# Attention values product: native fp32 for three key tiles, three products of rounded halves for the other three

## The chip, the cores and the metric

The kernel runs on 1 core of one Trainium2 chip. The metric is device time in microseconds (us), and the time before is the median of three runs. A profile is one execution that the hardware profiler recorded; its own time and its span are given beside the median, because durations are read from it.

Five engines run side by side, each through its own instructions in order: TensorE multiplies matrices (PE in the profile, with its weight loads on a row of their own, PEld), VectorE (DVE) and ScalarE (ACT) work on rows of 128 partitions, GpSimd (POOL) does small things, and SyncE (SP) issues the loads. They wait for each other by semaphores.

## The reference, cut to what matters

Two layers over 512 latent tokens and 256 context tokens of width 1024: first a pooling mixer, then attention, each followed by a squared-ReLU MLP. The change lies in the attention of the second layer. Eight query heads of width 128 share two key/value heads, and each latent query sees all 768 tokens:

```python
def attend(q, k, v):
    s = jnp.einsum('bqhgd,bkhd->bhgqk', q, k).astype(jnp.float32) * (HEAD_DIM ** -0.5)
    p = jax.nn.softmax(s, axis=-1).astype(v.dtype)
    return jnp.einsum('bhgqk,bkhd->bqhgd', p, v)
```

The last line is the one that the change touches: probabilities times values, summed over the 768 keys, in six key tiles of 128. All of it is fp32.

## The kernel before, in words

**Two ways to multiply in fp32.** TensorE takes fp32 operands natively (tiles of type F32), or in a rounded form (F32R). With rounded operands one product loses low bits, so the kernel splits an operand x into hi, x rounded by a copy on ScalarE, and lo = x - hi by a subtraction on VectorE, and adds three products, hi*hi + hi*lo + lo*hi. Almost every product of this kernel is made of three such products. The attention values product was not: it was native.

**The attention.** A step is one head h and one block t of 128 queries; there are 32 steps, head by head, four blocks to a head (`steps`, line 1189). A step goes through four functions:

- `s_scores` (line 1200): six rounded matmuls of 384 columns into the PSUM tile `pss` (two 512-column banks, from a pool of two, `psA`); VectorE takes the maximum of each row (line 1212), ScalarE the exponential with its sum (line 1213), into one of four row buffers. In the trace these four are called `gate`, `p`, `p` and `acc`, in the order t = 0, 1, 2, 3.
- `s_norm` (line 1217): VectorE's reciprocal (1219) and the scaling of the 128x768 row (1220).
- `s_turn` (line 1222): TensorE transposes the six 128x128 key tiles of the row, three at a time, into a PSUM tile `pspt` (line 1230), and ScalarE copies each three to `soft["t"]`, called `pT` in the trace (line 1231).
- `s_values` (line 1233), once for two steps, so 16 times: for 256 queries, six native matmuls (line 1241), one for each key tile kt, add values times probabilities into a PSUM tile `po`. The stationary operand is a 128x128 tile of the values, kept in rows 4 and 5 of `xr`; the moving one is 128x256 of `pT`. ScalarE and VectorE then store hi and lo of the result (lines 1242 and 1243).

`pspt`, `po` and `pq` (below) come from one pool, `psB`, of four 512-column PSUM tiles. A tile is given to its next user when the last reader has finished.

Beside the steps, `q_head` (line 1192) transposes the queries of a head through `pq` and splits them (1197, 1198), and the output weights are loaded and split in quarters of 512 columns (lines 126 and 129).

**What sets the order.** Each function is put at a due time written out by hand (`attention`, line 1281): step i has its scores at i + 0.2, its scaling at i + 1.3, its transposes at i + 3.1, and the values of a pair at i + 5.2 of its second step, in units of 2.7. So the values of a pair are due after the transposes of the step two later. From the program in this order a planner then fixes, by its own estimates, each engine's final order of instructions; it may put a transpose between two matmuls of the scores. In the run itself each engine follows that order strictly.

**Where the values come from.** Ahead of the attention, `kv_a` projects 128 tokens to keys and values in a `psq` tile, `kv_e` (line 1079) copies the value half with ScalarE into `xr` (line 1081) and starts the norm of the keys; `head_norm` (from line 1033) finishes the keys on VectorE. The token tiles come in the order 4, 5, 0, 1, 2, 3.

**The ramp.** The last query projections (`project`, line 1021, and `head_norm`, lines 1037 to 1051) overlap the first steps of the attention, between 678 and 697 us of the span. VectorE has both kinds of work there.

Of the kernel before, what the change touches and what calls it, by code (L numbers as in the profile page):

```python
# [9 lines left out]
F32 = mybir.dt.float32  # L10
F32R = mybir.dt.float32r
BF16 = mybir.dt.bfloat16
AF = mybir.ActivationFunctionType
ALU = mybir.AluOpType
# [3 lines left out]
P = 128  # L18
D = 1024
KT = D // P  # L20
LAT = 512
# [3 lines left out]
NT = TOK // P  # L25
# [30 lines left out]
def backbone(ctx: ExitStack, tc, x, c, ctx_in, c_ctx, w_ada, b_ada, g_mix_pre, g_mix_post,  # L56
# [3 lines left out]
    sy, ve, sc, gp, te = nc.sync, nc.vector, nc.scalar, nc.gpsimd, nc.tensor  # L60
# [9 lines left out]
    def residents(stack):  # L70
        pool = stack.enter_context(tc.tile_pool(name="residents", bufs=1, side="right"))
        return (pool.tile([P, NT, D], F32, name="xr"), pool.tile([P, 2, D], F32, name="gate"),
                pool.tile([P, D], BF16, name="junk"))

    xr, gate, junk = residents(held[0])
# [15 lines left out]
    rb = const.tile([P, 10240], F32R, name="rb")  # L91
# [642 lines left out]
    for n, t in enumerate(order):  # L734
        b = 55 + 3 * n
# [289 lines left out]
    def head_rstd(ps, nh):  # L1025
        ss, ms, r = sm_tile("ss"), sm_tile("ms"), sm_tile("rs")
        for h in range(nh):
            sc.activation(junk[:, 0:HD], ps[:, h * HD:(h + 1) * HD], AF.Square, accum_out=ss[:, h:h + 1])
        gp.tensor_scalar(out=ms[:, 0:nh], in0=ss[:, 0:nh], scalar1=1.0 / HD, scalar2=EPS, op0=ALU.mult, op1=ALU.add)
        gp.tensor_tensor(out=r[:, 0:nh], in0=ms[:, 0:nh], in1=nhalf[:, 0:nh], op=ALU.pow)  # L1030
        return r
# [39 lines left out]
            if cols == THIRDS:  # L1071
                tc.keep_in_program_order(z)

    values = lambda: xr[:, 4:6].rearrange("p t n -> p (t n)")[:, 0:1536].rearrange("p (t n) -> p t n", n=256)

    def kv_a(t):
        pj[t] = project(t, chunks[2])

    def kv_e(t):
        ps = pj[t]  # L1080
        sc.copy(values()[:, t, :], ps[:, 256:512])
        pj[t] = ps, head_rstd(ps, NKV)

    def kv_b(t):
# [26 lines left out]
    def last0(st, n, t):  # L1111
# [5 lines left out]
        if n % 2:  # L1117
            st.at([18.2, 28.6, 39][n // 2], norm_pair, t - 1, 1, 0, hH, hL, True, (True, True, False)[n // 2],
                  ((True, False, False, False, False, False, False, True), (True, True, True, False, False, False, True, True), (True, False, True, False, True, False, True, False))[n // 2])
        st.at([31.4, 36.6, 41.8, 47, 55, 60.2][n], kv_a, t)  # L1120
        st.at([36.874, 40.793, 45.993, 51.193, 59.193, 65.4][n], kv_e, t)
        st.at([36.9, 42.1, 47.3, 52.5, 60.5, 65.7][n], kv_b, t)
        st.at([44.9, 50.1, 57.151, 62.351, 70.351, 75.551][n], kv_c, t)
# [44 lines left out]
    soft = {}  # L1168

    def open_soft():  # L1170
        uheld[0].close()
        pool = uheld[0].enter_context(tc.tile_pool(name="soft", bufs=1))
        qs = pool.tile([P, 2 * 1024], F32R, name="qs")
        qTs.extend((qs[:, 1024 * i:1024 * i + 512], qs[:, 1024 * i + 512:1024 * i + 1024]) for i in range(2))
        soft["t"] = pool.tile([P, NT, LAT], F32, name="pT")
        ps = [pool.tile([P, TOK], F32, name=f"p{i}") for i in range(2)]
        soft["p"] = ps

# [43 lines left out]
    def s_turn(i):  # L1222
        _, t = steps[i]
        sl = slice(t * P, (t + 1) * P)
        p = pbuf(i % 4)
        for b in range(2):
            ps = psB.tile([P, 3, P], F32, tag="b", name="pspt")
            for j in range(3):
                k = 3 * b + j
                te.transpose(ps[:, j, :], p[:, k * P:(k + 1) * P], ident)  # L1230
            sc.copy(soft["t"][:, 3 * b:3 * b + 3, sl], ps)

    def s_values(i):
        h, t = steps[i]
        half = t // 2
        kv = h // 4
        hs = slice(kv * HD, (kv + 1) * HD)
        qs = slice(256 * half, 256 * half + 256)
        po = psB.tile([P, 512], F32, tag="b", name="po")
        for kt in range(NT):  # L1240
            te.matmul(po[:, 0:256], values()[:, kt, hs], soft["t"][:, kt, qs], start=(kt == 0), stop=(kt == NT - 1))
        sc.copy(oH[:, h, qs], po[:, 0:256])
        ve.tensor_tensor(out=oL[:, h, qs], in0=po[:, 0:256], in1=oH[:, h, qs], op=ALU.subtract)

# [36 lines left out]
    def attention(st, base, unit_t):  # L1281
        at = lambda i, fn, *args: st.at(base + unit_t * i, fn, *args)
        for i, (h, t) in enumerate(steps):
            if t == 0:
                at([-2, 3, 4.542, 7.928, 13.236, 15.602, 19.752, 23.755][h], q_head, h)
            at(i + 0.2, s_scores, i)
            at(i + 1.3, s_norm, i)
            at(i + 3.1, s_turn, i)
            if t % 2:
                at(i + 5.2, s_values, i)  # L1290
        raws, late = [], []
        at(1.1, open_soft)
        at(37.5, close_soft)
        at(7, lambda: wo[0].append(wo_unit(0, 0, raws)))
        at(11.386, lambda: wo[0].append(wo_unit(0, 1, raws)))
        for n in range(8):
            at(9.05 + 2 * n, lambda n: split(*raws[n // 4], True, n % 4), n)
        for kk in range(2):
            at((23.386, 25.741)[kk], lambda kk: late.append(raw_load(w_o[1, kk], rawp)), kk)
            at(37.6, lambda kk: wo[1].append(aring.place(late[kk], 512, raws)), kk)  # L1300
        at(37.812, lambda: split(*raws[2], q=0))
        at(38.427, lambda: split(*raws[2], q=1))
        at(37.814, lambda: split(*raws[2], q=2))
        at(37.815, lambda: split(*raws[2], q=3))
        at(39.191, lambda: split(*raws[3], q=0))
        at(39.192, lambda: split(*raws[3], q=1))
        at(39.193, lambda: split(*raws[3], q=2))
        at(45.691, lambda: split(*raws[3], q=3))
        at(39.281, gate_diag if False else gate_rows, 1, GT1, 0)
# [118 lines left out]
```

## Time and profile before

| | |
|---|---|
| median of 3 runs | 1182.24 us (1181.07 to 1183.31) |
| the profiled execution, its own time | 1180.16 us |
| its span | 1178.3 us |
| the attention's values products, first start to last end | 697.7 to 786.9 us |
| native matmuls in them | 96, in the trace as 192 records |

In the page of the profile, part 1 gives the busy time of each engine. In a row of a group stand the line, the engine, the operation, the output and inputs, the shapes and the count, then the total busy time in us and the mean of one in ns, then the idle time of the engine just before, and what ended it. In a timeline, a row holds the start in us, the duration in us and the same names; instructions of one kind that follow each other are merged (x12), and durations of TensorE's rows reach beyond the start of the next, as matmuls are pipelined: the pace is read from starts. A native matmul of 256 columns leaves two records, a rounded one leaves one.

### The profile page before, as it was taken

What the parts mean: (1) busy time and instruction counts of PE and PEld (TensorE: products, weight loads), DVE (VectorE), ACT (ScalarE), POOL (GpSimd) and SP (SyncE); (2) the same over time, 40 slices, a digit from 0 to 9 for tenths busy, and PEclk for the clock granted to TensorE, in tenths of its full rate; (3) what the DMA queues carried; (4) which work ended last, traced back from release to release, by engine and by line L of the source; (5) the groups of instructions that cost most, each with busy time, mean ns of one, the idle gap of its engine ahead of it and who ended that gap; (6) DMA issues with size and microseconds to landing.
All of it is one profiled execution on the core that took longest, in us unless ns stands there. A gap on an engine that the chain in (4) does not pass through costs nothing.

```text
span 1178.3 us, 15759 instructions
## 1 busy us (share of the span) xinstructions
PE 1145.3 (97%) x6074; PEld 990.0 (84%) x6074; DVE 922.6 (78%) x1491; ACT 627.6 (53%) x1072; POOL 68.8 (6%) x120
## 2 busy tenths in 40 slices
PE   5799999999999999999999999999899999999997
PEld 4579888998889988998888889988888888888886
DVE  3787778998988998896777587657687779778876
ACT  3776654555354445555585367752676346435522
POOL 2030000000000000000242200001100000000001
PEclk9999999999999999999999999999999999999999
DMA  8984213334433334343423101115234124214312
GB/s 340 378 290 172 72 72 117 135 142 144 143 143 143 132 120 145 110 147 135 179 72 108 37 1 36 37 50 203 101 120 170 47 97 143 108 36 143 107 38 106
DMA packets 25643, 147.84 MB, mean 125 GB/s; under 512 B 2736, under 2 KB 5216, under 8 KB 9824
## 3 DMA queue, kind: packets, MB, share of 16 engines
q1 hardware_dynamic: 25568, 146.84, 34.2%
q8 instruction: 48, 0.79, 0.3%
q14 instruction: 27, 0.22, 0.1%
HBM read 139.49 MB, written 7.34 MB: 125 GB/s over the span
## 4 chain that ended last, share of the span: by engine, by line
PE 48%; issue 43%; DVE 4%; POOL 2%; ACT 2%; DMA 1%; SPq 0%; POOLq 0%; DVEq 0%; ACTq 0%
PE pso L776 22%; PE psin L677 18%; PE psq L1021 3%; PE psin L553 3%; POOL rs L171 1%; PE psada L226 1%; POOL rs L1030 1%; ACT junk L156 1%; PE psm L420 1%; PE pspool L480 1%; DVE xr L328 1%; POOL ms L169 0%; DMA xr<-in_ctx 0%; DMA xr<-in_x 0%; DVE rows L268 0%
## 5 line engine op out<-in xcount | busy, mean ns | idle before, releaser
L776 PE MATMUL pso<-units,rb 128*128 128x512 f32 x1152 | 278.8, 392 | 0.0
L776 PEld LDWEIGHTS pso<-units,rb 128*128 128x128 f32 x1152 | 214.7, 188 | 41.1
L268 DVE SCALAR_TENSOR_TENSOR rows<-raw,cond,rows 128x256 f32<-128x256 f32 x280 | 126.8, 476 | 2.0
L788 DVE TENSOR_TENSOR acc<-acc,pso 128x512 f32<-128x512 f32 x129 | 85.2, 675 | 41.9 <-PE pso L776 41.7
L553 PE MATMUL psin<-ra,rb 128*128 128x512 f32 (+1 forms) x432 | 104.7, 342 | 2.4 <-ACT ra L363 1.6
L880 PE MATMUL pso<-units,pairs 128*128 128x512 f32 x336 | 82.3, 389 | 0.0
L553 PEld LDWEIGHTS psin<-ra,rb 128*128 128x128 f32 x432 | 70.2, 189 | 13.6 <-ACT ra L363 1.9
L553 PE MATMUL psin<-ra 128*128 128x512 f32 x256 | 80.6, 390 | 0.0
L880 PEld LDWEIGHTS pso<-units,pairs 128*128 128x128 f32 x336 | 63.1, 188 | 13.1
L884 DVE TENSOR_TENSOR acc<-acc,pso 128x512 f32<-128x512 f32 x72 | 48.7, 682 | 28.8 <-PE pso L880 28.8
L169 POOL TENSOR_SCALAR ms<-ss 128x1 f32<-128x1 f32 x20 | 10.0, 502 | 1001.3 <-ACT junk L156 989.2
L677 PE MATMUL psin<-ra,units 128*128 128x384 f32 x336 | 65.6, 337 | 0.4 <-ACT psin L689 0.4
L677 PE MATMUL psin<-sums,units 128*128 128x384 f32 x336 | 64.0, 336 | 0.0
L677 PEld LDWEIGHTS psin<-ra,units 128*128 128x128 f32 x336 | 59.9, 188 | 3.9 <-ACT psin L689 0.5
L677 PEld LDWEIGHTS psin<-sums,units 128*128 128x128 f32 x336 | 58.9, 188 | 1.6
L129 DVE TENSOR_TENSOR units<-raw,units 128x1024 fp32r<-128x1024 f32 (+2 forms) x49 | 55.0, 1150 | 5.9 <-ACT units L126 5.6
L126 ACT CAST units<-raw 128x1024 fp32r<-128x1024 f32 (+2 forms) x49 | 47.0, 995 | 17.9 <-PE pso L776 13.7
L553 PEld LDWEIGHTS psin<-ra 128*128 128x128 f32 x256 | 48.0, 188 | 10.0
L553 PE MATMUL psin<-rb 128*128 128x512 f32 (+1 forms) x144 | 52.6, 367 | 0.2 <-DVE rb L364 0.2
L786 ACT COPY acc<-pso 128x512 f32<-128x512 f32 x48 | 27.1, 586 | 48.3 <-PE pso L776 47.8
L1021 PE MATMUL psq<-units,ra 128*128 128x512 f32 x216 | 51.6, 392 | 0.0
L553 PE MATMUL psin<-rb,ra 128*128 128x512 f32 x128 | 49.8, 389 | 0.0
(250 smaller groups left out, 2318.3 us busy)
## 6 DMA issues: line engine op xcount, KB each, us to landing
raw<-in_w_ada SPq DMA_DIRECT2D x48, 1024.0 KB, 4.9
raw<-in_w_mlp_in SPq DMA_DIRECT2D x32, 1024.0 KB, 4.9
raw<-in_w_mlp_out SPq DMA_DIRECT2D x32, 1024.0 KB, 5.2
raw<-in_w_qkv SPq DMA_DIRECT2D x6, 1024.0 KB, 4.8
spill<-xr SPq DMA_DIRECT2D x10, 512.0 KB, 9.0
xr<-spill SPq DMA_DIRECT2D x10, 512.0 KB, 6.7
raw<-in_w_o SPq DMA_DIRECT2D x4, 1024.0 KB, 4.8
xr<-in_x SPq DMA_DIRECT2D x4, 512.0 KB, 4.2
```

Source lines behind the costliest of these rows:

```text
L126: a = sc.copy(hi, raw)
L129: b = ve.tensor_tensor(out=lo, in0=raw, in1=hi, op=ALU.subtract)
L156: z = sc.activation(junk[:, 0:src.shape[-1]], src, AF.Square, scale=float(D) ** -0.5, accum_out=ss)
L268: ve.scalar_tensor_tensor(out=r, in0=raw[:, k, :], scalar=cond[:, k, c:c + 1], in1=r, op0=ALU.mult, op1=ALU.add)
L553: te.matmul(ps[:, bank, o:o + ln], w[:, k, fs], rhs, start=start, stop=(k == KT - 1 and n == 2), skip_group_check=len(ks) < KT)
L677: te.matmul(bank, w[k], a[k], start=start and k == 0 and m == 0, stop=stop and k == 3 and m == 2, skip_group_check=True)
L776: te.matmul(pss[h][:, 0:cols[h][1]], a[:, f, ts_], w[:, f, cols[h][0]:sum(cols[h])], start=(n == 0 and not seeded[t]), stop=(n == len(seq) ...
L786: sc.copy(d, ps)
L788: ve.tensor_tensor(out=d, in0=d, in1=ps[:, 0:w], op=ALU.add)
L880: te.matmul(ps, a, w, start=(m == 0), stop=(m == len(seq) - 1))
L884: ve.tensor_tensor(out=M[n][:, t], in0=M[n][:, t], in1=ps, op=ALU.add)
L1021: te.matmul(ps, a[:, k, sl], w[:, k % 4, :], start=(k == 0 and n == 0), stop=(k == KT - 1 and n == 2))
```

## The change

Key tiles 0 to 2 stay native, with the same data as before. For key tiles 3 to 5 the product is made of rounded halves:

- `kv_e` writes the values of tokens 3, 4 and 5 (tiles of 128) as hi and lo into a free part of `rb`: a copy on ScalarE as before, and a new subtraction on VectorE.
- `s_turn`, for its second three key tiles, lets ScalarE's copy write hi instead of the full value, and adds a subtraction on VectorE from the same PSUM tile, 128x384, for lo.
- `s_values` has three native matmuls and then nine rounded ones in the place of the last three: vH*hi, vL*hi, vH*lo for each key tile.
- The buffers of the transposed probabilities grow from one tile of 6 x 512 columns to 3 x 512 native and 2 x 3 x 512 rounded.

```diff
-    values = lambda: xr[:, 4:6].rearrange("p t n -> p (t n)")[:, 0:1536].rearrange("p (t n) -> p t n", n=256)
+    values = lambda: xr[:, 4, 0:768].rearrange("p (t n) -> p t n", n=256)
+    vH = rb[:, 3072:3840].rearrange("p (t n) -> p t n", n=256)
+    vL = rb[:, 3840:4608].rearrange("p (t n) -> p t n", n=256)
...
     def kv_e(t):
         ps = pj[t]
-        sc.copy(values()[:, t, :], ps[:, 256:512])
+        if t < 3:
+            sc.copy(values()[:, t, :], ps[:, 256:512])
+        else:
+            sc.copy(vH[:, t - 3, :], ps[:, 256:512])
+            ve.tensor_tensor(out=vL[:, t - 3, :], in0=ps[:, 256:512], in1=vH[:, t - 3, :], op=ALU.subtract)
         pj[t] = ps, head_rstd(ps, NKV)
...
-        soft["t"] = pool.tile([P, NT, LAT], F32, name="pT")
+        halves = pool.tile([P, 2, 3, LAT], F32R, name="pTh")
+        soft["t"] = pool.tile([P, 3, LAT], F32, name="pT"), halves[:, 0], halves[:, 1]
...
-            sc.copy(soft["t"][:, 3 * b:3 * b + 3, sl], ps)
+            full, hi, lo = (z[:, :, sl] for z in soft["t"])
+            if b == 0:
+                sc.copy(full, ps)
+            else:
+                sc.copy(hi, ps)
+                ve.tensor_tensor(out=lo, in0=ps, in1=hi, op=ALU.subtract)
...
-        for kt in range(NT):
-            te.matmul(po[:, 0:256], values()[:, kt, hs], soft["t"][:, kt, qs], start=(kt == 0), stop=(kt == NT - 1))
+        full, hi, lo = soft["t"]
+        seq = [(values()[:, kt, hs], full[:, kt, qs]) for kt in range(3)]
+        seq += [(v[:, kt, hs], p[:, kt, qs]) for kt in range(3) for v, p in ((vH, hi), (vL, hi), (vH, lo))]
+        for n, (v, p) in enumerate(seq):
+            te.matmul(po[:, 0:256], v, p, start=(n == 0), stop=(n == len(seq) - 1))
```

In the order of the built program, the queues of SP and POOL are the same as before. TensorE's, VectorE's and ScalarE's differ only from the value copies on and up to the end of the attention.

## The prediction

> **What bounds the kernel now.** I read the page's busy times first, then the busy time of each engine by stages, and then TensorE's timeline in the attention.
>
> ```profile
> PE 1145.3 (97%) x6074; PEld 990.0 (84%) x6074; DVE 922.6 (78%) x1491; ACT 627.6 (53%) x1072; POOL 68.8 (6%) x120
> ```
>
> ```profile
> 690.00:700.00 10.00, 8.25 (x51) 7.65 (x52) 8.91 (x18) 6.89 (x17) 0.00 (x0) 1.00 0.00 0
> 700.00:787.00 87.00, 87.00 (x528) 80.55 (x527) 56.87 (x105) 60.50 (x137) 0.00 (x0) 1.00 0.07 25
> ```
>
> The columns of the stages are the stretch, its length, then busy time with counts of PE, PEld, DVE, ACT and POOL, the granted clock and the DMAs. From 700 to 787 us TensorE is busy without a gap at full clock, with VectorE at 65% (56.87 of 87) and ScalarE at 70%. So in the attention TensorE's own time sets the end, and each microsecond that its list gets shorter or longer goes to the span, as long as the others keep up. Between 690 and 700 it is the reverse: VectorE 89%, TensorE with holes. The change takes time from TensorE and gives work to VectorE, so both stretches have to be worked out.
>
> **The change part by part.**
>
> *TensorE, the values products.* The timeline shows the first group of six native matmuls and what follows it, and further down the last stretch of rounded matmuls of 256 columns with a weight load each:
>
> ```profile
> 697.73 2.76 PE L1241 MATMUL po<-pT,xr 128*128 128x256 f32 x12
> 700.32 0.82 PE L1230 MATMUL pspt<-ident,gate 128*128 128x128 f32 x6
> ...
> 828.41 5.40 PE L1266 MATMUL psy<-units,ra 128*128 128x256 f32 x43
> 833.64 0.28 PE L553 MATMUL psin<-ra,rb 128*128 128x256 f32 x1
> ```
>
> From start to start the six take 700.32 - 697.73 = 2.59 us, 0.432 for one. The rounded ones take (833.64 - 828.41) / 43 = 0.1216. A new group is 3 x 0.432 + 9 x 0.1216 = 1.296 + 1.094 = 2.39 us, so a group saves 0.20, and 16 groups save 3.2 us. The other end of the bound is the slowest group of this shape:
>
> ```profile
> L480 PE MATMUL pspool<-rb,ra 128*128 128x256 f32 x144 | 19.0, 287 | 0.2 <-DVE work L454 0.2
> ```
>
> 19.0 / 144 = 0.132 gives 9 x 0.132 = 1.19 and 1.7 us in all. I take 3.2, from the row where they stand back to back, as they will here.
>
> [...]
>
> *TensorE, more changes of kind.* Counted in the built order, TensorE goes over from native to rounded matmuls 33 times in this part before and 50 times after. What one costs is seen in two cycles of the attention, of which the first has three such changes (its scores are cut in two by transposes) and the second two:
>
> ```profile
> 729.08 2.75 PE L1241 MATMUL po<-pT,xr 128*128 128x256 f32 x12
> 731.67 0.49 PE L1230 MATMUL pspt<-ident,p 128*128 128x128 f32 x3
> 731.92 1.12 PE L1208 MATMUL pss<-rb,qs 128*128 128x384 f32 x5
> 732.88 0.49 PE L1230 MATMUL pspt<-ident,p 128*128 128x128 f32 x3
> 733.12 0.42 PE L1208 MATMUL pss<-rb,qs 128*128 128x384 f32 x1
> ...
> 735.09 2.75 PE L1241 MATMUL po<-pT,xr 128*128 128x256 f32 x12
> ...
> 741.55 2.76 PE L1241 MATMUL po<-pT,xr 128*128 128x256 f32 x12
> ...
> 747.56 2.76 PE L1241 MATMUL po<-pT,xr 128*128 128x256 f32 x12
> ```
>
> 735.09 - 729.08 and 747.56 - 741.55 are both 6.01 us. So the 17 changes cost nothing that shows; 0.
>
> *VectorE in the steady attention.* Each of the 32 steps gets one subtraction of 128x384 from PSUM. Its neighbours:
>
> ```profile
> L1212 DVE TENSOR_REDUCE sm<-pss 128x1 f32<-128x768 f32 x26 | 24.8, 955 | 13.8 <-PE pss L1208 13.7
> L1243 DVE TENSOR_TENSOR ra<-po,ra 128x256 fp32r<-128x256 f32 x16 | 6.8, 422 | 8.8 <-ACT ra L1242 8.8
> L1219 DVE RECIPROCAL sm<-sm 128x1 f32<-128x1 f32 x27 | 4.3, 159 | 7.1 <-ACT p L1213 3.6 <-ACT gate L1213 2.4 <-ACT acc L1213 1.2
> L1220 DVE TENSOR_SCALAR gate<-gate,sm 128x768 f32<-128x768 f32 x6 | 3.7, 620 | 0.2
> L1198 DVE TENSOR_TENSOR qs<-pq,qs 128x512 fp32r<-128x512 f32 x5 | 3.5, 691 | 0.8 <-ACT qs L1197 0.4
> L129 DVE TENSOR_TENSOR rb<-raw,rb 128x512 fp32r<-128x512 f32 x4 | 2.7, 684 | 0.0
> ```
>
> Half way between 422 and 691 ns is 0.557 us. Durations overlap a little: in the rows below the 128x512 subtraction starts 0.60 before the next instruction (694.37 to 694.97) and the scaling 0.53 (695.16 to 695.69), so by starts I count 0.08 less for each: 0.87 reduce, 0.19 reciprocal, 0.54 scaling, 0.48 the new one, 0.61 a split or a query head, 0.34 the output's lo. A cycle of two steps is then 2 x (0.87 + 0.19 + 0.54 + 0.48) + 0.61 + 0.34 = 5.1 us, 5.7 with a query head in it. TensorE's new cycles are 6.01 - 0.20 = 5.8 and, with a head (741.55 - 735.09 = 6.46), 6.26. VectorE goes to about 90% and still keeps up. What is queued behind the new subtraction is the next reduce or reciprocal; who waits for it is a tile of `psB`, which is now held 0.5 us longer, and the values. Both have room: the values of a pair are due after the transposes of the step two later, and in the trace the last transposes of the pair used at 741.55 were over by 735.09, 6 us earlier. I count 0 and keep the other end for the rivals.
>
> ScalarE's copies stay the same in number and size, only the output type is other (`ra` from `po` is a copy of that type already): 0.
>
> *VectorE in the ramp.* Here it has no slack. The rows follow each other without idle time:
>
> ```profile
> 693.77 0.68 DVE L1051 TENSOR_TENSOR acc<-work 128x512 f32<-128x512 f32 x1
> 694.37 0.68 DVE L1198 TENSOR_TENSOR qs<-pq,qs 128x512 fp32r<-128x512 f32 x1
> 694.97 0.24 DVE L1219 RECIPROCAL sm<-sm 128x1 f32<-128x1 f32 x2
> 695.16 0.62 DVE L1220 TENSOR_SCALAR acc<-acc,sm 128x768 f32<-128x768 f32 x1
> 695.69 0.61 DVE L1220 TENSOR_SCALAR gate<-gate,sm 128x768 f32<-128x768 f32 x1
> 696.22 2.01 DVE L1212 TENSOR_REDUCE sm<-pss 128x1 f32<-128x768 f32 x2
> ...
> 697.07 0.82 PE L1230 MATMUL pspt<-ident,acc 128*128 128x128 f32 x6
> ```
>
> The transposes at 697.07 need the scaled row `acc`, ready at 695.16 + 0.62 = 695.78: 1.3 us to spare. In the changed order two new subtractions and one reduce (it was behind the scaling) stand ahead of that scaling: 2 x 0.48 + 0.87 = 1.83 us. It ends at 697.61, and TensorE waits from 697.07 to about 697.65: +0.6 us. The lower bound is 0, if the two subtractions find gaps that the rows do not show, and the 1.3 to spare cover the reduce. The upper bound is 1.2: by full durations 2 x 0.557 + 0.955 = 2.07 stand ahead, 0.8 more than there is to spare, and 0.4 if the next reduce comes late as well. The exponentials that hold `pss` are not behind the new work, so the two holes of TensorE earlier in the ramp stay.
>
> *The values' halves.* Three subtractions of 128x256, 0.422 each. Two of them follow the first of these rows, the third falls in the stage of the last:
>
> ```profile
> 612.36 1.28 DVE L364 TENSOR_TENSOR ra<-acc,ra 128x512 fp32r<-128x512 f32 x2
> 618.61 0.42 DVE L1037 TENSOR_TENSOR work<-psq,rs 128x256 f32<-128x256 f32 x1 [4.97 <-POOL rs L1030]
> ```
>
> ```profile
> 640.00:660.00 20.00, 20.00 (x92) 16.46 (x91) 12.20 (x21) 8.12 (x34) 5.52 (x8) 1.00 0.29 107
> ```
>
> VectorE idles 4.97 us ahead of the norm at 618.61 and both fit there; in the stage of the third VectorE has 7.8 us of 20 free and TensorE none. 0; if that cover were gone, 3 x 0.42 = 1.3 us at the most.
>
> *Memory.* Native and rounded buffers stand in the same pool in the place of `units`; no load is added, and the queues of SP and POOL keep their order. 0.
>
> **The sum**: -3.2 + 0.6 = -2.6 us. Against the profiled execution that is a span of 1178.3 - 2.6 = 1175.7 and a time of 1180.16 - 2.6 = 1177.6. That execution lies 2.1 under the median of the runs, so against the median: 1182.24 - 2.6 = **1179.6 us**. With the bounds (-3.2 + 0 and -1.7 + 1.2) it is 1179.0 to 1181.7.
>
> **The rivals.**
>
> *VectorE becomes the pace (slower).* Take full durations in place of starts: 2 x (0.955 + 0.159 + 0.620 + 0.557) + 0.684 + 0.422 = 5.69, with a head 6.38; add the idle time that it can't avoid, since the reciprocal waits for ScalarE's exponential (7.1 us before 27 of them, 0.26 each, 0.53 a cycle): 6.2 and 6.9. Then TensorE's cycles of 5.8 and 6.26 are stretched by 0.4 and 0.65. Nine cycles hold a split, five of them with a head: 4 x 0.4 + 5 x 0.65 = 4.9, and the time is 1179.6 + 4.9 = 1184.5 us. It decides from the point where VectorE's cycle is longer than TensorE's 5.8; by starts it is 5.1 to 5.7, near that point. Against it speaks that a late VectorE has other work in place of those waits.
>
> *Weight loads set the pace of the rounded matmuls (slower).* Nine weight loads in place of three pairs:
>
> ```profile
> L480 PEld LDWEIGHTS pspool<-rb,ra x144: 186/192/193, 44.4 to 76.3; 128*128 128x128 f32 x144
> ```
>
> Were they not hidden, nine would take 9 x 0.192 = 1.73 in place of 1.296: +0.43 a group, +6.9 in all, 1182.24 + 6.9 + 0.6 = 1189.7 us. The 43 matmuls at 0.1216 speak against it: each has a load of its own. [...]
>
> *The gain is lost in the ramp (same).* If the late ramp is not made up and a second group waits as the first, the ramp costs 2 x 1.2 = 2.4 and -0.8 is left: 1181.4 us.
>
> *More than forecast (faster).* The ramp's wait is covered: -3.2, 1179.0 us.
>
> **How the numbers follow.** Forecast 0.60, VectorE's pace 0.18, weight loads 0.03, lost in the ramp 0.13, covered ramp 0.06. About 0.2% (2.4 us, 1179.9) is what a measurement here can tell from no change, and the forecast lies just beyond it. Of the forecast's 0.60 I give 0.37 to faster by more and 0.23 to within. Faster: 0.37 + 0.06 = 0.43. Same: 0.23 + 0.11 = 0.34. Slower: 0.18 + 0.03 + 0.02 = 0.23. The range is 1177.9 (1179.0 less the 1.1 by which the runs scatter) to 1185.6 (1184.5 plus 1.1); it leaves out the weight loads.
>
> **What would show it.** The profile of the changed kernel should have 9 rounded matmuls in about 1.09 us from start to start behind 3 native ones in 1.30; 32 subtractions of 128x384 near 557 ns; VectorE's busy time up by 32 x 0.557 + 3 x 0.42 = 19 us; TensorE without idle time after about 700 us; one new wait of the transposes of `acc` on VectorE near 697 us, of 0.6. Idle time of TensorE on VectorE in the steady cycles would show the first rival, matmuls 0.19 apart the second.

## The result, and the profile after

The changed kernel takes 1179.39 us (median of 16 runs, 1176.79 to 1180.2), the kernel before 1181.28 us (median of 16 runs beside them). The ratio is 0.9979, with a 95% interval of 0.9972 to 0.9987: 1.5 to 3.3 us faster, 2.5 in the middle. In a later session the ratio was 0.9977 (0.9967 to 0.9987). Two executions among the experiments, one of e3 (2324 us) and the profiled one of e4 (2944 us), took far longer than all the others and are in none of the ratios. The profiled execution of the changed kernel took 1178.74 us, its span 1177.0.

The page's busy times, and the stages (stretch, length, then busy time with counts of PE, PEld, DVE, ACT and POOL, granted clock, DMAs):

```profile
PE 1141.4 (97%) x6122; PEld 988.7 (84%) x6122; DVE 937.7 (80%) x1526; ACT 627.1 (53%) x1072; POOL 68.0 (6%) x120
```

```profile
690.00:700.00 10.00, 7.76 (x49) 7.01 (x50) 10.00 (x22) 6.89 (x17) 0.00 (x0) 1.00 0.01 2
700.00:785.00 85.00, 85.00 (x586) 81.48 (x585) 70.43 (x136) 60.49 (x139) 0.00 (x0) 1.00 0.08 26
```

From 700 us to the end of the attention TensorE still has no gap, and VectorE went from 65% to 83% (70.43 of 85). In the ten microseconds ahead of that VectorE is full and TensorE lost another 0.5 us. Those are the two sides of the change.

To measure the attention by itself, take the start of the last projection's 24 records and the start of the first `psy` matmul, which comes right behind the attention. Before, and then after, from TensorE's timeline (start, length, engine, line):

```profile
679.65 5.64 PE L1021 MATMUL psq<-units,ra 128*128 128x512 f32 x24
...
787.94 3.01 PE L1266 MATMUL psy<-ra 128*128 128x512 f32 x12
```

```profile
679.69 5.64 PE L1021 MATMUL psq<-units,ra 128*128 128x512 f32 x24
...
697.69 0.85 PE L1237 MATMUL pspt<-ident,acc 128*128 128x128 f32 x6 [0.45 <-DVE acc L1227]
698.37 1.46 PE L1256 MATMUL po<-pT,xr 128*128 128x256 f32 x6
699.48 1.42 PE L1256 MATMUL po<-pTh,rb 128*128 128x256 f32 x9
700.73 1.04 PE L1215 MATMUL pss<-rb 128*128 128x384 f32 x5
...
785.08 3.00 PE L1281 MATMUL psy<-ra 128*128 128x512 f32 x12
```

It took 787.94 - 679.65 = 108.29 us and now takes 785.08 - 679.69 = 105.39: **2.90 us less**. The first values mark a point in between. Up to them it was 697.73 - 679.65 = 18.08 and is 18.68 (+0.60); from them to `psy` it was 90.21 and is 86.71 (-3.50). A group of values lasts from 698.37 to 700.73, 2.36 us in place of 2.59.

Then 1.56 us come back. From the first `psy` to the end it was 1178.3 - 787.94 = 390.36 us and is 1177.0 - 785.08 = 391.92, though nothing was changed there. The stages around 844 us show where, after first and before second:

```profile
842.00:846.00 4.00, 3.78 (x17) 3.57 (x18) 3.14 (x5) 4.00 (x5) 0.00 (x0) 0.58 0.02 4
```

```profile
842.00:846.00 4.00, 2.14 (x17) 1.70 (x16) 3.20 (x7) 3.81 (x8) 0.00 (x0) 1.00 0.00 0
```

The last but two column is TensorE's granted clock. TensorE waits twice for 1.6 us just ahead of this point, in both kernels. After these waits the clock was 0.50 from 842.61 to 846.03 us in the profiled execution of after, and full in that of before. So the two profiled spans differ by 0.04 - 2.90 + 1.56 = -1.3 us, less than the change is worth. Whether this belongs to the change is asked below.

### The profile page after: what moved, and what is told of

Same layout as the page of the kernel before. It is cut to its first block, busy times and chain, and to the rows that moved or that the text cites. A ratio compares the mean times of both kernels' runs of the same rounds, so it can differ in the third digit from the quotient of the medians.

```text
span 1177.0 us, 15898 instructions
## 1 busy us (share of the span) xinstructions
PE 1141.4 (97%) x6122; PEld 988.7 (84%) x6122; DVE 937.7 (80%) x1526; ACT 627.1 (53%) x1072; POOL 68.0 (6%) x120
## 4 chain that ended last, share of the span: by engine, by line
PE 46%; issue 43%; DVE 4%; POOL 3%; ACT 2%; DMA 1%; SPq 0%; POOLq 0%; DVEq 0%; ACTq 0%
PE pso L776 22%; PE psin L677 18%; PE psin L553 3%; PE psq L1021 2%; POOL rs L171 1%; ACT junk L156 1%; POOL rs L1030 1%; PE psada L226 1%; POOL ms L169 1%; PE pspool L480 1%; DVE xr L328 1%; PE psm L420 0%; DMA xr<-in_ctx 0%; DMA xr<-in_x 0%; DVE rows L268 0%
```

## The experiments

The theory, from the prediction: TensorE's list sets the time behind the ramp, so rounding the halves is worth what the values' groups get shorter; VectorE's new subtractions cost only in the ramp. The main rival: VectorE becomes the pace. All runs, with the attention measured as above in each profile:

| run | ratio to before (95%) | last projection, first values, `psy` (us) | attention |
|---|---|---|---|
| before | 1 | 679.65, 697.73, 787.94 | 108.29 |
| after | 0.9979 (0.9972 to 0.9987) | 679.69, 698.37, 785.08 | 105.39 |
| e1 vector only | 1.0006 (0.9997 to 1.0014) | 680.56, 699.23, 789.47 | 108.91 |
| e2 tensor only | 0.9968 (0.9956 to 0.9980) | 680.72, 698.76, 785.46 | 104.74 |
| e3 subtract twice | 1.0001 (0.9992 to 1.0009) | 681.08, 701.89, 789.60 | 108.52 |
| e4 four tiles | 0.9967 (0.9956 to 0.9979) | | |
| e5 six tiles | 1.0022 (1.0013 to 1.0031) | 679.91, 702.10, 790.62 | 110.71 |
| e6 head 2 later | 0.9966 (0.9953 to 0.9978) | 682.18, 701.33, 787.10 | 104.92 |
| e7 four tiles, head 2 later | 0.9959 (0.9946 to 0.9971) | 679.91, 699.29, 783.88 | 103.97 |
| e8 four tiles again | 0.9964 (0.9950 to 0.9977) | 680.27, 700.80, 785.38 | 105.11 |
| e9 after again | 0.9977 (0.9967 to 0.9987) | 680.43, 699.12, 785.83 | 105.40 |
| e10 as e7 | 0.9967 (0.9958 to 0.9976) | 680.60, 700.02, 784.61 | 104.01 |
| e11 before again | | 680.62, 698.68, 788.90 | 108.28 |
| e12 before again | | 681.99, 700.04, 790.26 | 108.27 |

The attention of one kernel repeats to 0.04 us from profile to profile (108.29, 108.28, 108.27; 105.39, 105.40; 103.97, 104.01), while whole times scatter by a few microseconds. For a change that sits in one stage, the stage's own length is the finer scale. Before, after, e1 and e2 have the same work on TensorE up to the first values (only one set of transposes stands two matmuls earlier in before and e2), so the point in between can be compared as well. In e3, e6, e7, e8 and e10 one more block of scores stands ahead of it, in e5 two, and only the attention as a whole can be compared. The expectations of e1 and e2 count the attention from 674.72 us, 4.93 us earlier: their 113.2, 113.8, 109.7 and 110.3 are 108.3, 108.9, 104.8 and 105.4 on the table's scale.

**One half of the change at a time.** e1 gives VectorE its new work in the steps (not the three subtractions of the values' halves) and leaves TensorE's:

```diff
+        soft["lo"] = pool.tile([P, 3, LAT], F32R, name="pTl")
...
             sc.copy(soft["t"][:, 3 * b:3 * b + 3, sl], ps)
+            if b == 1:
+                ve.tensor_tensor(out=soft["lo"][:, :, sl], in0=ps, in1=soft["t"][:, 3:6, sl], op=ALU.subtract)
```

> The kernel before with one thing added: in each of the 32 steps VectorE also subtracts 128x384 into a spare buffer that nothing reads (values and products stay native fp32, kv_e as before). My theory (TensorE's list of work sets the time behind the ramp, VectorE's subtraction lies in its waits): only the ramp pays, +0.6 us over before (0 to 1.2), the attention from the last projection's start to the first psy goes from 113.2 to about 113.8 us, and no wait of PE on DVE stands behind 700 us. Rival (VectorE is the pace of the steady stage): 32 x 0.48 us of starts minus what slack covers, +4 to +5 us, with PE waiting on DVE in many cycles.

e2 gives TensorE its new matmuls and takes the subtraction in the steps away, so that its result leaves out the low part of the probabilities:

```diff
                 sc.copy(hi, ps)
-                ve.tensor_tensor(out=lo, in0=ps, in1=hi, op=ALU.subtract)
...
-... (vL, hi), (vH, lo))]
+... (vL, hi), (vH, hi))]
```

> The kernel after without the subtraction in s_turn; its third product reads the high half in place of the low half, so the low part of the probabilities is left out of the result, and TensorE does the same 3 native and 9 rounded matmuls per group. My theory: TensorE's gain alone, 3.2 to 3.5 us under before, with no ramp wait of 0.45 us on the scaling of acc, so the attention takes about 109.7 us (113.2 before, 110.3 after). Rival (the gain comes from another order of the work or is lost to a lower clock): no more than after's 2.5, and groups that do not last 2.36 us.

TensorE's waits in the ramp and the attention of e1, in us in total, times, longest:

```profile
PE pss L1209 <- ACT acc L1214: 1.6, 1, 1.6
PE pspt L1231 <- DVE acc L1221: 0.4, 1, 0.4
PE pss L1209 <- ACT p L1214: 0.4, 1, 0.4
```

e1 takes 108.91 us, 0.62 more than before. Nearly all of it is ahead of the first values (18.67 against 18.08), with the one new wait on the scaling of `acc`. From there it is 90.24, as before (90.21). e2 takes 104.74, 3.55 less than before, and its way to the first values is before's (18.04). The two parts add up: -3.55 + 0.62 = -2.93, and both together gave -2.90. The times agree (1.0006 and 0.9968). So TensorE's part is the whole gain and VectorE's part is a cost of the ramp alone; the rival's +4 to +5 for e1 is out.

**How much room VectorE has.** e3 does the new subtraction twice in each step of after.

```diff
-                ve.tensor_tensor(out=lo, in0=ps, in1=hi, op=ALU.subtract)
+                for _ in range(2):
+                    ve.tensor_tensor(out=lo, in0=ps, in1=hi, op=ALU.subtract)
```

> The kernel after with the 128x384 subtraction done twice in each step, same result. VectorE's list grows by 0.48 us a step, to about 6.06 us a pair of steps (6.66 with a head's 128x512) against TensorE's 5.79 (6.25). My theory (VectorE has about 0.6 us a pair to spare in after): it is now the pace, 8 x 0.27 + 8 x 0.41 + about 1.0 in the ramp = +6.4 us over after, +3.9 over before; PE waits on DVE in the steady stage. Rival (VectorE has much more room than I count): within 1 us of after. Rival (VectorE was the pace in after already): 32 x 0.48 = +15 us over after.

The attention takes 108.52 us, 3.13 more than after, and by the ratios it is 2.6 slower: half of what I expected, and far from the 15 of a VectorE that was the pace already. The first values come 20.81 - 18.68 = 2.13 later than in after, but in this order one more block of scores, 1.15 us, stands ahead of them. So the ramp pays about 1.0, as expected, and the steady stage 2.1 in place of 5.4. The stages of e3, and of after:

```profile
700.00:770.00 70.00, 68.93 (x463) 65.61 (x464) 68.17 (x141) 50.34 (x116) 0.00 (x0) 1.00 0.09 31
```

```profile
700.00:770.00 70.00, 70.00 (x481) 67.36 (x480) 62.15 (x119) 51.56 (x118) 0.00 (x0) 1.00 0.09 31
```

VectorE is at 97% (68.17 of 70), and still TensorE is idle for only 1.1 of 70. Nor does it wait on VectorE there, though I had expected that. Its one longer wait in this stage, 0.91 us up to 727.02, is for an exponential that ScalarE started at 725.97, right behind its copy of a head's queries; VectorE's maximum for it was done at 725.52. My count of VectorE's cycle was too long. The timeline of e3 in a stretch without idle time gives what an instruction takes from start to start:

```profile
707.33 0.94 DVE L1219 TENSOR_REDUCE sm<-pss 128x1 f32<-128x768 f32 x1
708.19 0.54 DVE L1244 TENSOR_TENSOR pTh<-pspt,pTh 128x384 fp32r<-128x384 f32 x1
708.65 0.15 DVE L1226 RECIPROCAL sm<-sm 128x1 f32<-128x1 f32 x1
708.73 0.67 DVE L1205 TENSOR_TENSOR qs<-pq,qs 128x512 fp32r<-128x512 f32 x1
709.31 0.60 DVE L1227 TENSOR_SCALAR gate<-gate,sm 128x768 f32<-128x768 f32 x1
709.84 0.68 DVE L129 TENSOR_TENSOR ra<-raw,ra 128x512 fp32r<-128x512 f32 x1
710.44 0.94 DVE L1219 TENSOR_REDUCE sm<-pss 128x1 f32<-128x768 f32 x1
```

The reduce takes 0.86, the new subtraction 0.46, the reciprocal 0.08 (I had counted 0.19), the scaling 0.53. A pair of steps is 2 x (0.86 + 0.46 + 0.08 + 0.53) + 0.34 = 4.2 us, and 0.6 more for each split or head in it: 4.8 and 5.4, where the prediction had 5.1 and 5.7, against TensorE's 5.8 to 6.3. The doubled subtraction brings 0.92: 5.1 to 6.3, level with TensorE only in the fullest pairs.

**More key tiles.** If TensorE's list is the time, each further tile that is rounded should be worth 0.07 x 16 = 1.1 us, until VectorE is in the way. Four tiles (e4, e8) and all six (e5):

```diff
-            ps = psB.tile([P, 3, P], F32, tag="b", name="pspt")
-            for j in range(3):
-                k = 3 * b + j
+            n = (2, 4)[b]
+            ps = psB.tile([P, 4, P], F32, tag="b", name="pspt")[:, 0:n]
+            for j in range(n):
+                k = 2 * b + j
...
```

> The kernel after with four of the six key tiles in rounded halves (2 native matmuls and 12 rounded a group; the transposes in groups of 2 and 4, so that the subtraction is 128x512; one of the p buffers moves to the free part of xr). TensorE: another 0.067 us a group, -1.1 us over 16 groups. VectorE: +0.12 us a step by the 128x512 row's starts, about 5.34 us a pair (5.94 with a head) against TensorE's 5.72 (6.18). My theory: TensorE is still the pace, -1.1 + up to 0.3 in the ramp = about 0.8 to 1.1 us under after, 3.3 to 3.6 under before. Rival (VectorE is so near the pace that any more shows): +1 to +4 us over after.

> The four-tile version once more, for its profile, whose execution was disturbed the first time: groups of 2 native and 12 rounded matmuls of about 2.29 us in place of after's 2.36, the attention from the last projection's rows to the first psy in 104.3 to 104.7 us in place of after's 105.4, no wait of PE on DVE in the steady stage.

```diff
-            full, hi, lo = (z[:, :, sl] for z in soft["t"])
-            if b == 0:
-                sc.copy(full, ps)
-            else:
-                sc.copy(hi, ps)
-                ve.tensor_tensor(out=lo, in0=ps, in1=hi, op=ALU.subtract)
+            hi, lo = (z[:, 3 * b:3 * b + 3, sl] for z in soft["t"])
+            sc.copy(hi, ps)
+            ve.tensor_tensor(out=lo, in0=ps, in1=hi, op=ALU.subtract)
...
```

> The kernel after with all six key tiles in rounded halves (18 rounded matmuls a group, two 128x384 subtractions a step, the p buffers in the freed part of xr). TensorE saves another 3.2 to 3.5 us over the 16 groups against after. VectorE carries the list of the run with the subtraction done twice: by its starts 4.20 + 0.93 + about 0.65 for heads and splits = 5.8 us a pair of steps, against TensorE's 6.0 in after and 5.8 here. My theory (VectorE is now level with TensorE): -3.3 from TensorE, +3.1 as the doubled subtraction cost, and up to 2 more since no slack is left to catch up: -0.2 to +1.8 us against after. Rival (only TensorE counts): -3.3 us against after, 0.995 of before. Rival (VectorE is strictly the pace, as in my first count): +5 us over after.

e8 is the same kernel as e4, and the profile of four tiles is read from it. Its timeline, and one of its waits:

```profile
700.80 1.03 PE L1257 MATMUL po<-pT,xr 128*128 128x256 f32 x4
701.48 1.78 PE L1257 MATMUL po<-pTh,rb 128*128 128x256 f32 x12
703.09 0.82 PE L1238 MATMUL pspt<-ident,gate 128*128 128x128 f32 x6
```

```profile
PE pss L1215 <- ACT p L1220: 1.2, 1, 1.2
```

The group is 703.09 - 700.80 = 2.29 us, as expected, 0.07 under after's. The attention, 105.11, is only 0.28 under after's. TensorE is busy 101.95 us of it, 1.0 less than after's 102.96, but idle 3.16 us and not 2.43: the order built for it has a wait of 1.2 us for an exponential in the ramp, where after has 0.45 for the scaling. I had allowed 0.3 for the ramp. The times (0.9967 and 0.9964) are 1.2 to 1.8 us under after's (0.9979 and 0.9977), with intervals that overlap after's.

With six tiles the timeline, TensorE's longest waits (the ramp's among them) and the stage are:

```profile
702.10 2.31 PE L1249 MATMUL po<-pTh,rb 128*128 128x256 f32 x18
704.25 0.49 PE L1234 MATMUL pspt<-ident,gate 128*128 128x128 f32 x3
```

```profile
PE pss L1212 <- ACT xr L1217: 3.0, 3, 1.7
PE pss L1212 <- ACT gate L1217: 2.5, 4, 0.9
```

```profile
700.00:770.00 70.00, 65.48 (x486) 63.26 (x485) 66.62 (x138) 47.98 (x113) 0.00 (x0) 1.00 0.09 31
```

The group is 2.15 us: 0.21 under after's, 0.119 for a matmul. So TensorE has 3.4 us less to do, and yet the attention is 110.71, 5.3 over after: TensorE is idle 8.7 us of it, against 2.4 in after. I had expected -0.2 to +1.8. The rival's +5 is met in number, with VectorE at 95%, but the trace does not show its mechanism, VectorE as the pace. One of TensorE's waits, with the rows of the other engines that lead up to it:

```profile
709.81 0.95 DVE L1216 TENSOR_REDUCE sm<-pss 128x1 f32<-128x768 f32 x1
...
711.92 0.82 PE L1234 MATMUL pspt<-ident,xr 128*128 128x128 f32 x6
...
712.45 0.86 ACT L1236 CAST pTh<-pspt 128x384 fp32r<-128x384 f32 x2 [1.00 <-PE pspt L1234]
713.20 0.92 ACT L1217 ACTIVATE xr<-pss,sm 128x768 f32<-128x768 f32 x1
...
714.25 1.31 PE L1212 MATMUL pss<-rb,qs 128*128 128x384 f32 x6 [0.86 <-ACT xr L1217]
```

VectorE's maximum for this exponential was done at 710.76. ScalarE began the exponential at 713.20, because its copies of a row's transposes come first in its order, and these waited 1.00 us for TensorE's own transposes. In all five waits for an exponential behind 705 us the maximum had been done 0.8 to 2.4 us before the exponential began, and the exponential stood right behind a copy of transposes (four times) or of a head's queries (once). So in these waits it is ScalarE's order that holds TensorE up. Whether the planner chose that order because VectorE's list had grown is not shown. Nor is it shown why e3, with the same subtractions in number and size, took 2.2 us less. One difference is that with six tiles both `pspt` tiles of a step are held until VectorE has read them; I have not taken that apart from the change of order, and it stays open.

**The wait in the ramp.** e6 moves the query transposes of head 2, which head 2 needs only at step 8, behind the scaling of `acc`:

```diff
-                at([-2, 3, 4.542, 7.928, 13.236, 15.602, 19.752, 23.755][h], q_head, h)
+                at([-2, 3, 5.6, 7.928, 13.236, 15.602, 19.752, 23.755][h], q_head, h)
```

> The kernel after with one due time changed: the transposes of head 2's queries, with their copy and subtraction, come at 5.6 steps in place of 4.542, so the 128x512 subtraction no longer stands ahead of the scaling of acc, and ScalarE's copy of those queries no longer stands ahead of the exponential into acc. My theory: the new wait of TensorE on acc's scaling (0.45 us) goes, and 0.48 us of the 1.57 us that it waits for the exponential: 0.9 us under after, with 17.8 us from the last projection's last group of rows to the first values in place of 18.7. Rival (the wait comes from the two new subtractions and only moves, or the other order of the rest costs as much): within 0.3 us of after.

The wait on `acc` is gone and the attention is 104.92, 0.47 under after. The second half of what I expected did not come: TensorE's wait for the exponential is still there, 1.5 us. The exponential starts earlier, but the moved transposes stood ahead of it on TensorE too, so TensorE arrives earlier by as much. By the times e6 (0.9966) is under after (0.9979), with overlapping intervals.

e7 and e10 are four tiles with this due time.

> The four-tile version with head 2's queries at 5.6 steps as well. If both effects hold and add up: 0.9 us under the four-tile version, some 4.5 to 4.8 us under before (0.9960). If the ramp's gain is only given back later: no better than the four-tile version (0.9967).

> The four-tile version with head 2's queries later, beside the kernel after on the same chip. From the profiles of the attention, 103.97 us against 105.39: 1.4 us under after, 4.0 to 4.8 us under before. If the two gains were chance: no more than 0.5 us under after.

The attention is 103.97 and 104.01: 1.4 under after, 1.1 under e8 and 4.3 under before. Against e6's 104.92 the four tiles bring 0.95 of their 1.1, now that the wait of 1.2 is gone; a wait of 0.2 for the scaling of `acc` is left. Beside after on one chip (e9) e10 had 1177.11 us (1176.58 to 1180.09, 10 runs) against 1178.93 (1177.38 to 1179.5, 9 runs). In the two sessions it is 0.9959 and 0.9967 of before. It is the best version found; that it beats after is shown by the profiles' attention, while the intervals of the times overlap in the session that they share.

**The half clock.** Three executions more, one of after and two of before, for the low clock near 844 us.

> The kernel after once more, for two things. First, whether the half clock that its first profile shows after TensorE's two waits of 1.6 us near 840 us belongs to the kernel or to that one execution: my theory is the execution, so the attention again takes 105.4 us from the last projection's rows to the first psy, and the stretch from there to the end takes 390.3 us (as in the runs without the low clock) or 391.9 us (with it), either way. Rival (the change causes it): the half clock is there again at the same place. Second, its time beside the next run on the same chip.

> The kernel before once more, one look. In its first profile the stretch from the first psy to the end took 390.4 us with no low clock near 840 us, and its time was 2.1 us under the median of its runs. My theory (about 1.6 us of what its runs scatter by is the half clock behind the two waits near 843 us): if this execution shows the low clock, the stretch takes 391.9 us and the time is near 1182; if not, 390.3 and near 1180. Rival (the low clock comes with the change): no low clock here, whatever the time. The attention takes 108.3 us either way.

> As the run before it: with the low clock near 843 us 391.9 us from the first psy to the end and a time near 1182 us, without it 390.3 and near 1180; the attention 108.3 us either way.

The first of these rows is e11, a run of the kernel before; the others are e7 and e10, two executions of one kernel:

```profile
846.00:850.00 4.00, 3.78 (x19) 3.57 (x19) 3.14 (x5) 3.99 (x5) 0.00 (x0) 0.57 0.00 0
```

```profile
842.00:846.00 4.00, 4.00 (x23) 4.00 (x22) 3.14 (x3) 2.96 (x3) 0.00 (x0) 0.57 0.01 4
```

```profile
842.00:846.00 4.00, 3.81 (x31) 3.81 (x32) 3.13 (x5) 3.73 (x4) 0.00 (x0) 1.00 0.02 4
```

Before has the half clock in e11 and in e12, and there it takes 1180.8 - 788.90 = 391.9 and 1182.1 - 790.26 = 391.8 us from `psy` to the end, against 390.36 in its first profile. After has it both times (e9: 391.87). One kernel shows it in e7 (391.7) and not in e10 (390.3). Six of the 13 profiles read here have it (after, e5, e7, e9, e11 and e12). So it belongs to the execution and not to the change, and it costs 1.5 us when it comes. The rival, that it comes with the change, is out. The times of the two new executions of before are 1182.65 and 1183.97; I had expected both near 1182. The second reaches the last projection 2.34 us later than the first profile of before; its clock was 0.70 from 44 to 48 us and 0.88 from 48 to 52, where the first had 1.00.

## Why the prediction was right, step by step

The forecast was 1179.6 us; the median is 1179.39. The sum was -2.6; the attention shows -2.9 and the ratio -2.5. The mechanism and each term hold. That the two times lie 0.2 apart is partly luck: the forecast starts from a median of three runs, 1182.24, and the median of 16 is 1181.28, from which the same sum gives 1178.7.

- **The values products (-3.2): right, a little small.** -3.50 in the profile of after, -3.55 alone in e2. The mis-sized term is the rounded matmul: 0.1194 (2.15 / 18 in e5) where I took 0.1216 from `psy`; 9 x 0.0022 x 16 = 0.3. The bound from the pooling's 0.132 was far off. What I said the rows would show within a group, 1.30 us for the native part and 1.09 for the rounded, was wrong: they show 1.11 and 1.25. Only a whole group from start to start can be read there. Three rounded products at 0.119 are 83% of a native one's 0.432.
- **17 more changes of kind (0): right.** e2 has them all, and its 3.55 is 16 x 0.22, the groups' own gain.
- **VectorE in the steady attention (0): right.** No wait of TensorE on VectorE stands behind 700 us, and e1 adds the work at 90.24 against 90.21. VectorE is busy 83% to 785 us and 89% to 770, near the "about 90%". But the room was larger than I counted: by starts a cycle takes 4.8 or 5.4 us and not 5.1 or 5.7, and with twice the new work, in e3, the steady stage paid 2.1 us and not 5.4. By the groups of VectorE (the new subtraction 0.551 where I interpolated 0.557), the idle time ahead of the reduce went from 13.8 to 4.9, of the reciprocal from 7.1 to 1.4:

```profile
L1219 DVE TENSOR_REDUCE sm<-pss 128x1 f32<-128x768 f32 x25 | 23.9, 954 | 4.9 <-PE pss L1215 4.5
L1243 DVE TENSOR_TENSOR pTh<-pspt,pTh 128x384 fp32r<-128x384 f32 x28 | 15.3, 551 | 2.5 <-ACT pTh L1242 2.5
L1226 DVE RECIPROCAL sm<-sm 128x1 f32<-128x1 f32 x26 | 4.2, 160 | 1.4 <-ACT p L1220 0.5 <-ACT acc L1220 0.3 <-ACT gate L1220 0.2
```

  That is what speaks against the first rival: it added waits as if they had to stay, and they were filled.
- **The ramp (+0.6): right in place and size.** The scaling of `acc` started at 695.16 and starts at 696.94, 1.78 later (1.83 forecast), behind two new subtractions and a reduce:

```profile
692.43 0.55 DVE L1243 TENSOR_TENSOR pTh<-pspt,pTh 128x384 fp32r<-128x384 f32 x1
...
694.89 0.55 DVE L1243 TENSOR_TENSOR pTh<-pspt,pTh 128x384 fp32r<-128x384 f32 x1
695.36 0.68 DVE L1205 TENSOR_TENSOR qs<-pq,qs 128x512 fp32r<-128x512 f32 x1
695.95 0.21 DVE L1226 RECIPROCAL sm<-sm 128x1 f32<-128x1 f32 x2
696.08 0.93 DVE L1219 TENSOR_REDUCE sm<-pss 128x1 f32<-128x768 f32 x1
696.94 0.60 DVE L1227 TENSOR_SCALAR acc<-acc,sm 128x768 f32<-128x768 f32 x1
```

  The page calls the wait 0.45 and the first values are 0.60 later. A wait is counted from the modelled end of the last matmul, and without it the transposes would have begun ahead of that end, as the values at 698.37 begin 0.17 ahead of the end of the row before them (697.69 + 0.85). So these waits on TensorE cost a little more than their rows say: 0.60 for 0.45 here, 0.59 for 0.44 in e1.
- **The values' halves and memory (0): right.** The last projection starts at 679.69, where it started at 679.65.
- **VectorE's busy time (+19): it is +15.1.** I added durations, though I had noted that they overlap by 0.08: 32 x 0.46 + 3 x 0.34 = 15.7.
- **The rivals.** VectorE as the pace is out by e1. A second subtraction of 128x384 a step brings VectorE to 97% (e3) and 95% (e5), and it costs time, but TensorE's waits on exponentials in those steady stages come out of ScalarE's order; no run here shows VectorE itself as the pace. Weight loads as the pace is out: 0.119 us a matmul in e5, each with a load of its own; these loads take 0.19 us in after. A gain lost in the ramp is out here, but e8 shows that it can happen: its ramp ate 0.8 of 1.1.

The profiled execution of before lay 2.1 us under the median of three runs and 1.1 under that of 16. e11 shows what such a difference can be made of. Its time is 2.49 over the first profile: 0.97 ahead of the last projection, and 1.54 behind `psy`, the half clock.

## What to carry to other kernels

Split a change into what it takes from the engine without gaps and what it gives to the engine with gaps, and look for the stretch in which the second has none: here 1% of the span, the ramp, took back a sixth of the gain. Measure a change of a few parts in a thousand by the length of its own stage, which repeated to 0.04 us, and not by the span of two profiles. Idle time of an engine that waits for its inputs in the middle of a cycle was room here, not a cost to be added to its work. And when a wait ends on an engine, look at what stood ahead in that engine's order, as in e5, before naming the busiest engine as the cause.

## What the runs showed of the hardware

Around 840 us TensorE paused twice for 1.6 us in both kernels (1.60 and 1.63 in before, 1.60 and 1.64 in after), with 1.53 us of matmuls in between. In six of the 13 profiles it then went on at half clock (0.50 from 842.61 to 846.03 us in after), which costs 1.5 us, and in the others at full clock, as in the first profile of before. One and the same kernel did both, in e7 and in e10.

The length of the half clock and its places show a step. In the trace of before the clock was 0.50 from 17.76 to 21.17 and from 31.41 to 34.83 us, in that of after from 16.59 to 20.00 and from 842.61 to 846.03. Each lasts 3.41 us, and within one trace these changes lie whole multiples of 3.41 us apart, 241 of them between 20.00 and 842.61. Cut into stretches of that length with the edges at the changes, TensorE was busy in after for 1.81 and 1.57 us of the two stretches ahead of the half clock near 844 us. In the first profile of before, without it, one stretch there was busy for 1.53 us, and the two beside it for 3.05 and 2.21. For e5, e7, e9, e11 and e12, with the half clock, my estimate from the changes of the clock in their stages and the pauses of before is 1.5 to 1.8 us of each of the two; for e1, e2, e3 and e6, without it, 1.53 us of one and at least 2.1 of those beside it. So in these profiles the half clock goes with where the edges of such stretches fall on the two pauses, and that differs between executions of one kernel. What decides it is not shown: near 44 us in e11 it came behind 2.15 busy us in the four from 40 to 44, and in the first profile of before, with 2.33 there, it did not come.

The half clock near 844 us explains 1.5 us of the scatter of these times, and the first 50 us some more. The stage of e11 there:

```profile
44.00:48.00 4.00, 4.00 (x29) 3.61 (x33) 2.55 (x8) 0.43 (x1) 0.00 (x0) 0.57 1.01 334
```

In the first profile of before the clock was 1.00 in this stage, and e11 came 0.97 us later to the last projection. In e11 TensorE was busy throughout with 29 records, in the first profile for 3.82 us with 46.
